# Stick-breaking attention inside a decoder block: the mask moves into the scan, and eight residual passes move behind the attention stage

## The chip, the cores and the metric

The kernel runs on one core of a Trainium2 chip. The metric is the device time of one execution in microseconds (us). The engines named below are TensorE (PE, matmuls; its weight loads are listed as PEld), VectorE (DVE), ScalarE (ACT), GpSimd (POOL) and SyncE (SP, which here only issues DMAs). Each engine works through its own queue of instructions in order; an instruction that waits holds up everything behind it on that engine, and nothing on the others unless they need its result.

## The reference

One decoder layer on 512 tokens of width 1024, in float32: a half-step SwiGLU feed-forward (width 2816), a token-mixing sublayer, and a second half-step feed-forward. Each is modulated by shift, scale and gate vectors from a conditioning vector, and followed by a LayerNorm over `alpha * x + gate * sublayer`. The token-mixing sublayer runs two branches from one input projection: stick-breaking attention (16 heads of 64) and a causal depthwise convolution of 31 taps. The two are projected, merged with sigmoid gates and projected again.

The change lies in the attention. Its core is

```
z = (q @ k.T) * scale
mask = s_idx < t_idx                      # strictly earlier tokens only
log_keep = where(mask, log_sigmoid(-z), 0)
between = reversed_cumsum(log_keep) - log_keep
w = where(mask, exp(log_sigmoid(z) + between), 0)
out = w @ v
```

So the weight of key `s` for query `t` is `sigmoid(z[t,s])` times the product of `sigmoid(-z[t,j])` over all `j` with `s < j < t`, and zero for `s >= t`.

## The kernel before

Tokens lie in four tiles of 128, the width in eight chunks of 128. Nearly all products are made in three matmuls: each float32 operand is split into a rounded high part and the remainder (`whi`/`wlo`, `uh`/`ul`, ...), and high*high, high*low and low*high are summed in PSUM.

The work runs in stages. The first feed-forward (with the modulation vectors beside it) ends at about 390 us. Then q, k, v and the convolution's inputs for the first heads are projected. From 423 to about 722 us the **attention stage** runs 64 units (8 pairs of heads x 2 heads x 4 query tiles `tb`) in a software pipeline. Step `i` of its loop (line 725) emits

- `att_scores(i)`: three matmuls into `z`; ACT writes `nb = sigmoid(-z)` (L629) and `be = sigmoid(z)` (L630); DVE runs a reversed multiplicative scan over `nb` (L631) that uses a constant tile `future`; POOL zeroes the masked part of `be` in its diagonal block with an affine select (L634) and multiplies `be` by the shifted `nb` (L636);
- some tasks of the input projection for later heads and for the convolution (`advance`), each a half of one weight tile;
- `att_values(i - 3)`: the products with v into `po` (L669 to L671);
- `att_transpose(i - 2)`: PE transposes of `be` into `pw` (L646), then ACT and DVE split them into `wTh` and `wTl` (L649, L650);
- two or three convolution taps on DVE (`bg`, L525), and on every fourth step one of the eight **slow** passes.

The slow passes come from `finish_x(1)` (line 302): over each of the four token tiles of the normalised residual `x`, POOL multiplies by a row `ln1_g * alpha` (four passes), and then adds a row `ln1_b * alpha` (four passes); L313 in the profile. The first pass of each four also fetches its row: a DMA on SP's queue (L100) that broadcasts 4 KB to 128 partitions of one of the three `raw` buffers, and an ACT multiplication by alpha (L307). The result is needed only when the sublayer's residual is added, near 930 us.

Weights of this sublayer come through `load_added` (line 125): SP loads a `raw` tile (3 buffers, shared with the two rows above), ACT rounds it into `whi` (L129) and writes `-whi` into `wlo` (L130), and a DMA on POOL's queue adds the source to `wlo` in flight (L131). `whi` and `wlo` have five buffers each, so a new weight is rounded when PE has finished with the one five before it.

After the attention, `parts_t(ysb)` splits the attention output (ACT L750, DVE L751), and the **first projection part** (loop at line 843, 40 tasks: gate `ga`, output projection `ysb`, half of gate `gb`, to 831 us) uses PE while DVE finishes the remaining taps. Then come the convolution's LayerNorm (`conv_normalize`, whose transposes L771 need every channel's last tap), its swish, its projection `ycv`, the merge and the output projection. The second feed-forward fills the rest.

The order of the instructions on each engine is not the program order as such. The kernel library's planner takes the trace of the program, and at each point gives an engine the earliest-traced instruction that it holds to be ready by its own cost estimates; buffers are handed out in that order too. `keep_in_program_order` ties one instruction behind the instruction traced just before it on the same engine, and nothing more: what follows in the program may still be put ahead of it, and it may be put ahead of everything else. It is used on the taps and on the slow passes' POOL instructions, not on the DMA and the ACT instruction that fetch a row.

Of the kernel before, what the change touches and what calls it, by code (L numbers as in the profile page):

```python
# [7 lines left out]
F32 = mybir.dt.float32  # L8
F32R = mybir.dt.float32r
BF16 = mybir.dt.bfloat16  # L10
AF = mybir.ActivationFunctionType
ALU = mybir.AluOpType
PSUM = bass.MemoryType.PSUM

P = 128
S = 512
D = 1024
KC = D // P
NT = S // P
# [11 lines left out]
LAG = 2  # L31
# [7 lines left out]
QSCALE = 0.125  # L39
# [3 lines left out]
def decoder_block(ctx: ExitStack, tc: tile.TileContext, a: dict, out: bass.AP):  # L43
    nc = tc.nc

    core = ctx.enter_context(tc.tile_pool(name="core", bufs=1))
# [3 lines left out]
    def open_pool(name, side="left", space=None):  # L50
        kw = {"space": space} if space is not None else {"side": side}
        cm = tc.tile_pool(name=name, bufs=1, reuse_waits="tile", **kw)
        return cm, cm.__enter__()

    def close_pool(cm):
        cm.__exit__(None, None, None)
# [7 lines left out]
    def bank(name, tag="ps"):  # L64
        return banks["pool"].tile([P, 512], F32, tag=tag, name=name, bufs=banks["bufs"][tag])
# [7 lines left out]
    ones = core.tile([P, P], F32, tag="uf", name="ones", bufs=2)  # L73
# [3 lines left out]
    ones_r = core.tile([P, P], F32R, name="ones_r")  # L77
    nc.vector.tensor_copy(ones_r, ones)

    future = core.tile([P, S], BF16, name="future")  # L80
    nc.gpsimd.memset(future[:, 0 : S - P], 0.0)
    nc.gpsimd.affine_select(future[:, S - P : S], ones, [[1, P]], ALU.is_ge, 0.0, base=0, channel_multiplier=-1)
    mhalf = core.tile([P, 1], F32, name="mhalf")
    nc.gpsimd.memset(mhalf, -0.5)

# [73 lines left out]
    def bg(n):  # L159
        for _ in range(min(n, len(background))):  # L160
            background.pop(0)()
# [140 lines left out]
    def finish_x(which):  # L302
        row = {}

        def fetch(v):
            row[v] = raw_tile(a[f"ln{which}_{v}"].broadcast_to([P, D]))
            nc.scalar.mul(row[v], row[v], ALPHA)  # L307

        def apply(t, v):
            if t == 0:  # L310
                fetch(v)
            op = nc.gpsimd.tensor_mul if v == "g" else nc.gpsimd.tensor_add
            tc.keep_in_program_order(op(x_t[t], x_t[t], row[v]))  # L313

        return [lambda t=t, v=v: apply(t, v) for v in "gb" for t in range(NT)]
# [184 lines left out]
    slow = finish_x(1)  # L500
# [6 lines left out]
    at_cm, ap_ = open_pool("mixa", "left")  # L507
# [104 lines left out]
        return [(fetch if t == 0 else None, lambda t=t: block(t)) for t in range(NT)]  # L612


    unit = {}

    def att_scores(i):
        j, hh, tb = i // 8, (i // 4) % 2, i % 4
        (qh, ql), (kh, kl) = qk[j, "q"], qk[j, "k"]
        rs = slice(hh * DH, (hh + 1) * DH)  # L620
        n = (tb + 1) * P
        tsl = slice(tb * P, (tb + 1) * P)
        z = bank("z", "z")
        nc.tensor.matmul(z[:, :n], qh[rs, tsl], kh[rs, :n], start=True, stop=False)  # L624
        nc.tensor.matmul(z[:, :n], qh[rs, tsl], kl[rs, :n], start=False, stop=False)
        nc.tensor.matmul(z[:, :n], ql[rs, tsl], kh[rs, :n], start=False, stop=True)
        nb = ap_.tile([P, S], F32, tag="nb", name="nb", bufs=2)
        be = ap_.tile([P, S], F32, tag="be", name="be", bufs=LAG + 1)
        nc.scalar.activation(nb[:, :n], z[:, :n], AF.Sigmoid, scale=-QSCALE)  # L629
        nc.scalar.activation(be[:, :n], z[:, :n], AF.Sigmoid, scale=QSCALE)  # L630
        nc.vector.tensor_tensor_scan(  # L631
            nb[:, 1:n][:, ::-1], nb[:, 1:n][:, ::-1],
            future[:, S - n + 1 : S][:, ::-1], 1.0, ALU.mult, ALU.max)
        nc.gpsimd.affine_select(be[:, n - P : n], be[:, n - P : n], [[-1, P]], ALU.is_gt, 0.0, base=0,  # L634
                                channel_multiplier=1)
        nc.gpsimd.tensor_mul(be[:, 0 : n - 1], be[:, 0 : n - 1], nb[:, 1:n])  # L636
        unit[i] = be

    def att_transpose(i):
        tb = i % 4  # L640
        n = (tb + 1) * P
        be = unit[i]
        pw = bank("pw", "pw")
        for sb in range(tb + 1):
            ss = slice(sb * P, (sb + 1) * P)
            nc.tensor.transpose(pw[:, ss], be[:, ss], ident)  # L646
        wh = ap_.tile([P, S], F32R, tag="wTh", name="wTh", bufs=2)
        wl = ap_.tile([P, S], F32R, tag="wTl", name="wTl", bufs=2)
        nc.scalar.copy(wh[:, :n], pw[:, :n])  # L649
        nc.vector.tensor_sub(wl[:, :n], pw[:, :n], wh[:, :n].bitcast(F32))  # L650
        unit[i] = (wh, wl)
# [3 lines left out]
    def att_values(i):  # L655
        j, hh, tb = i // 8, (i // 4) % 2, i % 4
        vh, vl = vq[j // 2]
        wh, wl = unit.pop(i)
        rs = slice(hh * DH, (hh + 1) * DH)
        vs = slice((j % 2) * P + hh * DH, (j % 2) * P + (hh + 1) * DH)  # L660
        tsl = slice(tb * P, (tb + 1) * P)
        if tb == 0:
            heads["po"] = bank("po", "po")
            if hh == 0:
                ysb.append(yp.tile([P, S], F32, tag="yF", name=f"yF{j}", bufs=KC))
        po = heads["po"]
        for sb in range(tb + 1):
            ss = slice(sb * P, (sb + 1) * P)
            nc.tensor.matmul(po[0:DH, tsl], vh[:, sb, vs], wh[:, ss], start=(sb == 0), stop=False)  # L669
            nc.tensor.matmul(po[0:DH, tsl], vh[:, sb, vs], wl[:, ss], start=False, stop=False)  # L670
            nc.tensor.matmul(po[0:DH, tsl], vl[:, sb, vs], wh[:, ss], start=False, stop=(sb == tb))  # L671
        if tb == NT - 1:
            nc.scalar.copy(ysb[j][rs, :], po[0:DH, :])
# [41 lines left out]
    def advance(to):  # L715
        nonlocal done, fetched
        while done < to:
            while fetched < min(done + AHEAD, len(tasks)):
                if tasks[fetched][0]:
                    tasks[fetched][0]()  # L720
                fetched += 1
            tasks[done][1]()
            done += 1

    for i in range(units + LAG + 1):
        if i < units:
            advance(max([done] + [x + 1 for x in range(done, len(tasks)) if need[x] <= i // 8]))
            att_scores(i)
        advance((i + 1) * len(tasks) // (units + LAG + 1))
        if i > LAG:  # L730
            att_values(i - LAG - 1)
        if LAG <= i < units + LAG:
            att_transpose(i - LAG)
        bg(int((i + 1) * CONV_PACE) - int(i * CONV_PACE))
        if i % 4 == 3 and slow:
            slow.pop(0)()
    close_pool(at_cm)

    t_cm, mp = open_pool("mixt", "left")
# [23 lines left out]
    def conv_normalize(t):  # L763
        tsl = slice(t * P, (t + 1) * P)
        st = bp.tile([P, 2, 6], F32, tag="cst", name="cst", bufs=2)
        n = [gp.tile([P, S], F32, tag="g", name="cn", bufs=NH_BUF) for _ in range(2)]
        pts = []
        for h in range(2):
            pt = bank("pt")
            for c in range(4):  # L770
                nc.tensor.transpose(pt[:, c * P : (c + 1) * P], cacc[4 * h + c][:, tsl], ident)  # L771
            nc.vector.bn_stats(st[:, h, :], pt)
            pts.append(pt)
        mv = bp.tile([P, 2], F32, tag="cmv", name="cmv", bufs=2)
        nc.vector.bn_aggr(mv, st)
        ve = bp.tile([P, 1], F32, tag="cve", name="cve", bufs=2)
        nc.vector.tensor_scalar_add(ve, mv[:, 1:2], EPS)
        rstd = bp.tile([P, 1], F32, tag="crs", name="crs", bufs=2)
        nc.gpsimd.tensor_tensor(rstd, ve, mhalf, ALU.pow)
        for h in range(2):  # L780
            nc.vector.tensor_scalar(n[h], pts[h], mv[:, 0:1], rstd, ALU.subtract, ALU.mult)
        normed[t] = n
# [47 lines left out]
    def advance_b(n):  # L830
        nonlocal done, fetched
        for _ in range(n):
            while fetched < min(done + AHEAD, len(queue)):
                if queue[fetched][0]:
                    queue[fetched][0]()
                fetched += 1
            queue[done][1]()
            done += 1
# [4 lines left out]
    for i in range(len(first_part)):  # L843
        advance_b(1)
        bg(min(n1, i + 1) * taps // n1 - min(n1, i) * taps // n1)
    assert not background
    conv_normalize(0)
    advance_b(1)
# [130 lines left out]
```

## Time and profile before

| | us |
|---|---|
| three runs | 1327.76, 1330.25, 1333.49 (median 1330.25) |
| the profiled execution, its own time | 1328.88 |
| its span in the trace | 1327.2 |
| PE busy in the span | 1292.2 |
| DVE, ACT, POOL busy in the span | 750.8, 524.6, 559.7 |

The profile lists instructions with their start and duration in us from the span's start. "Idle before" and a name behind `<-` give the time for which an engine did nothing ahead of an instruction, and the instruction or DMA that ended it. The granted clock (PEclk) is the share of full speed at which TensorE was allowed to run; a stretch at 0.50 takes twice as long for the same matmuls. The ends of matmuls are modelled, so neighbouring matmuls overlap in the list.

### The profile page before, as it was taken

Reading aid. Unit: us, or ns where it says so; the run is one execution under the profiler, and the core shown is the slowest. Engines: PE = TensorE matmul, PEld = TensorE weight load, DVE = VectorE, ACT = ScalarE, POOL = GpSimd, SP = SyncE. Lnnn points to the kernel's source line nnn. Section 1 sums busy time; section 2 is a strip of 40 time slices with the busy share of each in tenths; the row PEclk is TensorE's granted clock in tenths of the full one; section 3 lists DMA queues with packets and bytes.
Section 4 is the critical chain, followed back from the end, with each engine's and each line's share of the span. In section 5 each row is a group of like instructions: output and inputs, shape, how many; then the busy total and the mean of one; then the engine's idle time right before and its main releaser. Section 6 shows DMA issues by size and latency. Waiting matters only on the chain.

```text
span 1327.2 us, 16780 instructions
## 1 busy us (share of the span) xinstructions
PE 1292.2 (97%) x6444; PEld 1071.2 (81%) x6444; DVE 750.8 (57%) x1017; ACT 524.6 (40%) x794; POOL 559.7 (42%) x392
## 2 busy tenths in 40 slices
PE   6899999999999999999999999999999999999997
PEld 4688888888889878788778888878898888888885
DVE  7886885255462858766676876545672000025545
ACT  2233312222256555556556444852542222222220
POOL 2464535644222554534442111133264566564434
PEclk9999999999999989999999999999999999999999
DMA  9668886333327564655566989293273333323311
GB/s 356 217 211 314 293 293 215 103 96 96 95 81 171 123 150 96 159 112 118 121 135 135 191 193 200 51 225 109 77 272 100 101 106 101 117 96 96 96 64 63
DMA packets 57713, 197.36 MB, mean 149 GB/s; under 512 B 6673, under 2 KB 6817, under 8 KB 57633
## 3 DMA queue, kind: packets, MB, share of 16 engines
q1 hardware_dynamic: 47808, 160.63, 36.6%
q0 software_dynamic: 9824, 35.66, 16.4%
q8 instruction: 50, 0.82, 0.2%
q14 instruction: 31, 0.25, 0.1%
HBM read 194.17 MB, written 2.10 MB: 148 GB/s over the span
## 4 chain that ended last, share of the span: by engine, by line
PE 84%; DVE 8%; DMA 3%; issue 2%; ACT 1%; POOL 1%; SPq 0%; DVEq 0%; POOLq 0%; ACTq 0%
PE y L354 19%; DVE ada L188 3%; PE z L624 1%; DVE cacc L525 1%; PE pw L646 1%; PE glub L143 1%; PE ga L143 1%; PE ga L145 1%; PE ysb L145 1%; PE ga L144 1%; PE ysb L144 1%; PE ysb L143 1%; PE q L143 1%; PE glub L144 1%; PE glub L145 1%
## 5 line engine op out<-in xcount | busy, mean ns | idle before, releaser
L113 POOL TENSOR_TENSOR wlo<-raw,whi 128x1024 fp32r<-128x1024 f32 x88 | 224.8, 2561 | 239.0 <-ACT whi L112 233.5
L112 ACT CAST whi<-raw 128x1024 fp32r<-128x1024 f32 x144 | 149.6, 1046 | 265.3 <-DMA raw<-in_gu 45.2
L136 POOL TENSOR_TENSOR raw<-raw,mod_g 128x1024 f32<-128x1024 f32 x52 | 130.0, 2502 | 146.9 <-DMA raw<-in_dn 83.7
L525 DVE SCALAR_TENSOR_TENSOR cacc<-h,cv_w,cacc 128x512 f32<-128x512 f32 x232 | 179.7, 833 | 0.0
L129 ACT CAST whi<-raw 128x1024 fp32r<-128x1024 f32 x68 | 71.1, 1048 | 129.1 <-PE ysb L144 23.4
L113 DVE TENSOR_TENSOR wlo<-raw,whi 128x1024 fp32r<-128x1024 f32 x56 | 106.2, 1896 | 24.2 <-ACT whi L112 24.2
L354 PE MATMUL y<-whi,sh 128*128 128x512 f32 x352 | 113.8, 390 | 0.0
L354 PE MATMUL y<-wlo,sh 128*128 128x512 f32 x352 | 113.7, 389 | 0.0
L354 PE MATMUL y<-whi,sl 128*128 128x512 f32 x352 | 113.6, 389 | 0.0
L188 DVE SCALAR_TENSOR_TENSOR ada<-ada,crow 128x512 f32<-128x512 f32 x96 | 97.9, 1067 | 20.9 <-DMA ada<-in_ada_t 15.4
L418 DVE TENSOR_TENSOR sl<-sF,sh 128x512 fp32r<-128x512 f32 x44 | 45.3, 1031 | 85.3 <-ACT sh L417 85.3
L417 ACT CAST sh<-sF 128x512 fp32r<-128x512 f32 x44 | 27.1, 623 | 144.9 <-PE y L354 132.1
L131 POOL DMA_DIRECT2D wlo<-in_w_in x44 | 38.4, 872 | 98.9 <-ACT wlo L130 92.9
L636 POOL TENSOR_TENSOR be<-be,nb 128x127 f32<-128x127 f32 (+1 forms) x64 | 50.1, 783 | 68.7 <-DVE nb L631 55.1
L354 PEld LDWEIGHTS y<-whi,sl 128*128 128x128 f32 x352 | 66.1, 188 | 13.7
L354 PEld LDWEIGHTS y<-wlo,sh 128*128 128x128 f32 x352 | 66.1, 188 | 13.7
L354 PEld LDWEIGHTS y<-whi,sh 128*128 128x128 f32 x352 | 66.1, 188 | 13.5
L130 ACT ACTIVATE wlo<-whi 128x1024 fp32r<-128x1024 f32 x68 | 71.9, 1061 | 0.7
L650 DVE TENSOR_TENSOR wTl<-pw,wTh 128x128 fp32r<-128x128 f32 (+1 forms) x64 | 31.1, 485 | 52.8 <-ACT wTh L649 52.7
L634 POOL TENSOR_SCALAR_AFFINE_SELECT be<-be 128x128 f32<-128x128 f32 x64 | 40.9, 639 | 41.0 <-ACT be L630 40.6
L631 DVE TENSOR_TENSOR_SCAN nb<-nb,future 128x127 f32<-128x127 f32 (+1 forms) x64 | 53.4, 835 | 3.4 <-ACT nb L629 3.4
L221 DVE SCALAR_TENSOR_TENSOR acc<-ada,silu_c,acc 128x1024 f32<-128x1024 f32 x21 | 41.6, 1981 | 15.8 <-DMA ada<-in_ada_w 15.6
(494 smaller groups left out, 3376.4 us busy)
## 6 DMA issues: line engine op xcount, KB each, us to landing
raw<-in_gu SPq DMA_DIRECT2D x80, 512.0 KB, 3.6
raw<-in_w_in SPq DMA_DIRECT2D x48, 512.0 KB, 3.6
raw<-in_dn SPq DMA_DIRECT2D x44, 512.0 KB, 3.5
wlo<-in_w_in POOLq DMA_DIRECT2D x44, 512.0 KB, 6.0
ada<-in_ada_t SPq DMA_DIRECT2D x32, 512.0 KB, 5.3
ada<-in_ada_w SPq DMA_DIRECT2D x24, 512.0 KB, 5.0
ada<-in_ada SPq DMA_DIRECT2D x32, 256.0 KB, 6.0
raw<-in_gu_first SPq DMA_DIRECT2D x8, 512.0 KB, 6.6
```

What stands on the lines that cost most here:

```text
L112: nc.scalar.copy(hi, raw)
L113: lo_eng.tensor_sub(lo, raw, hi.bitcast(F32))
L129: nc.scalar.copy(hi, raw)
L130: nc.scalar.mul(lo, hi.bitcast(F32), -1.0)
L136: nc.gpsimd.tensor_mul(raw, raw, G)
L143: nc.tensor.matmul(ps[:, c0:c1], wh[:, ks], mov(uh, k)[:, c0:c1], start=(k == 0), stop=False)
L188: nc.vector.scalar_tensor_tensor(raw[:, qs], raw[:, qs], 1.0, crow[:, qs], ALU.mult, ALU.mult, accum_out=parts[:, q : q + 1])
L354: nc.tensor.matmul(acc[t][h][:, c0 - h * 512 : c1 - h * 512], st[:, tsl], wt[:, c0:c1], start=(k == 0 and i == 0 and c0 % 512 == 0), stop= ...
L418: nc.vector.tensor_sub(sl, sF[f], sh.bitcast(F32))
L525: ins = nc.vector.scalar_tensor_tensor(o, hv, cv_w[:, j, i : i + 1], o, ALU.mult, ALU.add)
L631: nc.vector.tensor_tensor_scan(nb[:, 1:n][:, ::-1], nb[:, 1:n][:, ::-1], future[:, S - n + 1 : S][:, ::-1], 1.0, ALU.mult, ALU.max)
L636: nc.gpsimd.tensor_mul(be[:, 0 : n - 1], be[:, 0 : n - 1], nb[:, 1:n])
```

## The change

Four edits.

1. The constant tile of the scan holds a one at the query's own token and zeros elsewhere (`own_token`, built with `is_equal`), where `future` held ones at the own token and everything behind it. The scan starts from 0 instead of 1. Running from the last key towards the first, its state is `max(state * nb, own_token)`: it stays 0 over the keys behind the query, becomes 1 at the query's own token and is multiplied by `nb` from there on. The product `be * nb` so is zero wherever the mask is, and the affine select (L634) is dropped.
2. `nb` and `be` are no longer taken from rings of 2 and 3 buffers of 512 columns. There is one `nb` and one `be` for each query tile, 128, 256, 384 and 512 columns wide, kept over the whole stage, so each is used every fourth unit. The total size is the same.
3. The last column of each `be` is set to zero once, before the stage, by four small memsets on POOL; ACT writes `be` without that column.
4. The slow passes are no longer emitted in the attention loop but in the first projection part, one after every second task (the first 16 of its 40).

The number of matmuls for a score is three before and after.

```diff
-    future = core.tile([P, S], BF16, name="future")
-    nc.gpsimd.memset(future[:, 0 : S - P], 0.0)
-    nc.gpsimd.affine_select(future[:, S - P : S], ones, [[1, P]], ALU.is_ge, 0.0, base=0, channel_multiplier=-1)
+    own_token = core.tile([P, S], BF16, name="own_token")
+    nc.gpsimd.memset(own_token[:, 0 : S - P], 0.0)
+    nc.gpsimd.affine_select(own_token[:, S - P : S], ones, [[1, P]], ALU.is_equal, 0.0, base=0, channel_multiplier=-1)
...
+    past = [ap_.tile([P, (tb + 1) * P], F32, name=f"nb{tb}") for tb in range(NT)]
+
+    weights = [ap_.tile([P, (tb + 1) * P], F32, name=f"be{tb}") for tb in range(NT)]
+    for tb in range(NT):
+        nc.gpsimd.memset(weights[tb][:, (tb + 1) * P - 1 :], 0.0)
     unit = {}
...
-        nb = ap_.tile([P, S], F32, tag="nb", name="nb", bufs=2)
-        be = ap_.tile([P, S], F32, tag="be", name="be", bufs=LAG + 1)
+        nb = past[tb]
+        be = weights[tb]
         nc.scalar.activation(nb[:, :n], z[:, :n], AF.Sigmoid, scale=-QSCALE)
-        nc.scalar.activation(be[:, :n], z[:, :n], AF.Sigmoid, scale=QSCALE)
+        nc.scalar.activation(be[:, : n - 1], z[:, : n - 1], AF.Sigmoid, scale=QSCALE)
         nc.vector.tensor_tensor_scan(
             nb[:, 1:n][:, ::-1], nb[:, 1:n][:, ::-1],
-            future[:, S - n + 1 : S][:, ::-1], 1.0, ALU.mult, ALU.max)
-        nc.gpsimd.affine_select(be[:, n - P : n], be[:, n - P : n], [[-1, P]], ALU.is_gt, 0.0, base=0,
-                                channel_multiplier=1)
+            own_token[:, S - n + 1 : S][:, ::-1], 0.0, ALU.mult, ALU.max)
         nc.gpsimd.tensor_mul(be[:, 0 : n - 1], be[:, 0 : n - 1], nb[:, 1:n])
         unit[i] = be
...
         bg(int((i + 1) * CONV_PACE) - int(i * CONV_PACE))
-        if i % 4 == 3 and slow:
-            slow.pop(0)()
     close_pool(at_cm)
...
     for i in range(len(first_part)):
         advance_b(1)
         bg(min(n1, i + 1) * taps // n1 - min(n1, i) * taps // n1)
+        if i % 2 and slow:
+            slow.pop(0)()
```

## The prediction

> **What bounds the kernel now.** I read the engines' totals first, then stretches around the stages that the change touches, then what PE waited for between 400 and 1000 us.
>
> ```profile
> PE 1292.2 (97%) x6444; PEld 1071.2 (81%) x6444; DVE 750.8 (57%) x1017; ACT 524.6 (40%) x794; POOL 559.7 (42%) x392
> ...
> 425.00:485.00 60.00, 59.71 (x369) 1.00 0.65 145
> 485.00:490.00 5.00, 2.49 (x16) 0.85 0.62 166
> 490.00:495.00 5.00, 5.00 (x16) 0.50 0.68 105
> 495.00:500.00 5.00, 5.00 (x26) 0.97 0.28 70
> 500.00:723.00 223.00, 221.76 (x1369) 1.00 0.58 124
> 723.00:831.00 108.00, 108.00 (x478) 1.00 0.88 190
> ...
> PE po L669 <- ACT wTh L649: 2.1, 1, 2.1
> PE po L670 <- DVE wTl L650: 1.3, 3, 0.5
> PE ga L143 <- ACT h L564: 0.7, 1, 0.7
> ```
>
> The first row is busy time by engine; the next six are stretch, length, PE busy (instructions), granted clock, DMA share and GB/s; the last three are who waited for whom: us in all, times, longest. PE is the bound: in the whole attention stage it is idle for 0.29 + 2.51 + 1.24 us, and POOL is nowhere named as the one that PE waits for. So this change, which takes nothing off PE, can win at most those gaps and the clock that one of them costs. Most of it is one place, so I followed that place across the queues:
>
> ```profile
> 479.37 5.28 DMA raw<-in_ln_b
> ...
> 484.67 1.06 ACT L307 ACTIVATE raw<-raw 128x1024 f32<-128x1024 f32 x1 [4.05 <-DMA raw<-in_ln_b]
> ...
> 487.66 0.57 ACT L649 CAST wTh<-pw 128x512 fp32r<-128x512 f32 x1
> ...
> 488.28 0.27 PE L669 MATMUL po<-wTh,vh 128*64 128x128 f32 x1 [2.06 <-ACT wTh L649]
> ```
>
> The second row of the residual passes is fetched in mid-attention. ACT stands 4.05 us in front of L307 until the row has landed; a weight's two conversions and the `wTh` cast (487.66) are queued behind it, and PE runs dry for 2.06 us, and right behind that comes its longest wait for `wTl` (the 0.5 above, 0.45 unrounded): the 2.51 of the stretch. Then the granted clock is down: (0.15 + 0.50 + 0.03) x 5 = **3.4 us** of work lost. A slow-pass row load, not the affine select, is what this stage pays for.
>
> [...]
>
> **The change part by part.**
>
> ```profile
> L634 POOL TENSOR_SCALAR_AFFINE_SELECT be<-be 128x128 f32<-128x128 f32 x64 | 40.9, 639 | 41.0 <-ACT be L630 40.6
> L636 POOL TENSOR_TENSOR be<-be,nb 128x127 f32<-128x127 f32 (+1 forms) x64 | 50.1, 783 | 68.7 <-DVE nb L631 55.1
> ...
> L313 POOL TENSOR_TENSOR n<-n,raw x8: 2360/2682/2850, 424.2 to 552.2; 128x1024 f32<-128x1024 f32 x8
> ...
> 472.25 1.41 DVE L525 SCALAR_TENSOR_TENSOR cacc<-h,cv_w,cacc 128x512 f32<-128x512 f32 x2
> 475.12 4.35 DVE L525 SCALAR_TENSOR_TENSOR cacc<-h,cv_w,cacc 128x512 f32<-128x512 f32 x2
> 476.08 2.84 POOL L313 TENSOR_TENSOR n<-n,raw 128x1024 f32<-128x1024 f32 x1
> ```
>
> *The affine select* (L634): 64 x 639 ns = 40.9 us leave POOL. The multiplication behind it waits 55.1 us for DVE's scan anyway, and PE waits for neither: 0 on the path. If that cover were gone, it would be 0.64 us of a unit's latency, not of throughput.
>
> *Scan, mask constant, one column less, buffers*: the scan is the same instruction on the same sizes with another start value; one column of 128 to 512 on ACT is nothing beside the 438 ns of L630; `nb` and `be` come back every fourth unit in place of every second and third, which can only take waits away, and no wait for them shows. 0.
>
> *The four memsets* stand once on POOL, where their tiles' memory was the first stage's:
>
> ```profile
> 389.23 0.23 POOL L563 MEMSET h<- 128x30 f32 x3
> 392.14 0.83 DVE n L273
> 396.39 0.91 POOL L131 DMA_DIRECT2D wlo<-in_w_v  x1 [4.29 <-ACT wlo L130]
> ```
>
> Four at 0.08 us each; the last reader of that memory (DVE's normalisation) is done at 392.97, and POOL idles for 4.29 us until 396.39. 0. Without that idle time the weight DMA behind them would be 0.3 us late, for products that start at 411 us.
>
> *The passes leave the attention.* DVE's taps stand still while POOL runs a pass: two taps took 4.35 us around the pass at 476 us, against 1.41 us just before, so 2.94 us. That delays the scan and `wTl`, and it explains the two other short waits for `wTl` (0.29 at 446 us, the idle time of 425 to 485; 0.55 at 558 us, which with the 0.7 of `ga` is the 1.24 of 500 to 723; each right behind a pass): -0.84 us. With the `ln_b` row the stall goes: -2.51 us and -3.4 us. The first row (`ln_g`, below) held ACT for 7.64 us, but at 415 to 423 us, before any unit, and PE had v products to do: 0.
>
> *Where they go.* A pass is tied only behind the POOL instruction traced before it. In the new place that is the weight DMA fetched one weight ahead, so pass 1 may follow the second weight's DMA, pass 8 the ninth's:
>
> ```profile
> 700.72 0.88 POOL L131 DMA_DIRECT2D wlo<-in_w_sb  x1 [2.36 <-ACT wlo L130]
> 723.51 0.86 POOL L131 DMA_DIRECT2D wlo<-in_w_in  x1 [5.94 <-ACT wlo L130]
> 746.62 0.87 POOL L131 DMA_DIRECT2D wlo<-in_w_in  x1 [4.23 <-ACT wlo L130]
> ```
>
> Counting the weights, three passes still fall into the attention's tail (behind 700.7, 710.7, 716.7 us) and five between 724 and 750 us. Three of eight passes cost 3/8 x 0.84 = +0.3 us. POOL itself idles 4 to 6 us ahead of each of these DMAs, more than a pass takes: 0. On DVE the five cost 5 x 2.94 = 14.7 us, and this is the cover:
>
> ```profile
> DVE ga L799 <- PE ysb L145: 16.6, 6, 5.0
> ...
> 823.73 0.69 DVE L530 TENSOR_TENSOR cacc<-cacc,cacc 128x512 f32<-128x512 f32 x1
> ...
> L771 PEld LDWEIGHTS pt<-ident,cacc x32: 138/141/143, 831.0 to 844.5; 128*128 128x128 f32 x32
> ```
>
> DVE waits 16.6 us in all for PE's `ysb` in this part, and has its last tap 6.6 us (831.0 - 824.4) before PE's transposes ask for it: 23.2 us of slack against 14.7. 0.
>
> *The two row loads move too*, through SP's queue and the three `raw` buffers. In order of tracing, `ln_g` comes between the second and third weight of the new part and takes the buffer free at 681.9 us; `ln_b` comes between the sixth and seventh and takes the one at 721.8.
>
> ```profile
> 681.91 0.33 SPq L100 DMA_DIRECT2D raw<-in_w_in  x1
> 721.79 0.33 SPq L100 DMA_DIRECT2D raw<-in_w_sb  x1
> DMA to landing us min/median/max: 3.7/6.0/10.4
> DMA to landing us min/median/max: 3.6/5.3/6.5
> ...
> 412.55 10.45 DMA raw<-in_ln_g
> 686.44 0.58 ACT L673 COPY yF<-po 64x512 f32<-64x512 f32 x1 [2.23 <-PE po L671]
> 687.04 0.27 ACT L649 CAST wTh<-pw 128x128 fp32r<-128x128 f32 x1
> 690.23 0.22 PE L669 MATMUL po<-wTh,vh 128*64 128x128 f32 x1
> 723.84 4.27 ACT L750 CAST ph<-yF 128x512 fp32r<-128x512 f32 x8
> L143 PE MATMUL ysb<-ph,whi x64: 388/389/390, 727.9 to 808.8; 128*128 128x512 f32 x64
> ```
>
> The two "to landing" rows are the three `ln_g` and the three `ln_b` loads of the kernel. Say L307 goes into ACT's 2.23 us gap, which begins at 684.2 us. With a landing of 5.3 us ACT is free at 681.9 + 5.3 + 1.06 = 688.3, casts the output copy (0.58) and `wTh` (0.27), done by 689.1; PE asks at 690.23: 0. Break-even is a landing of 6.4 us; at 10.45 it is 4.0 us of idling and, as at 488, 3.4 us of clock: +7.4. So 0 to 7.4; I take 0, since four of the six landings are under 6.4. `ln_b` lands about 727.1, while ACT does the eight casts of L750 (traced earlier, so preferred when ready) until 728.1: 0. If L307 stands ahead of them, the first cast (4.27 / 8) and its remainder (0.69, as DVE's operation of that size at 823.73) come 1.06 + 0.53 + 0.69 us behind the landing against 727.9: +1.5 us at 5.3, and +6.6 + 3.4 = +10.0 at 10.45. I take 0. Weights lose nothing: with one or, briefly, two of three raw buffers held, a weight's load mostly goes out two weights ahead, 11 us (four weights lie 23.1 us apart between 723.5 and 746.6), and the slowest of these six loads of the same 512 KB took 10.4.
>
> **Sum**: -2.51 - 3.4 - 0.84 + 0.3 = -6.4 us on the profiled execution of 1328.88, that is 1322.4. The median of the three runs is 1.4 us above that execution, so I state **1324**.
>
> **The rivals.**
>
> *A. The stall only moves to the attention's tail.* `ln_g` lands late at 682 us, with ACT in front of it. For: two of six landings exceed 6.4 us, and both early loads met ACT waiting. Against: 681.9 is in a stretch of moderate DMA load (0.58 share from 500 to 723). -6.4 + 7.4 = +1.0: **1331**.
>
> *B. Slower: ACT stands at the handoff.* At 722 to 734 us ACT must cast the attention output before any `ysb` product. If `ln_b`'s L307 is put ahead of L750, PE idles from a landing of 3.8 us on, and the whole is slower than before if that load takes over about 7 us. At 10.45: -6.4 + 10.0 = +3.6, **1334**. For: the planner put L307 at most 1.2 us behind the issue at 479. Against: earlier-traced work goes first.
>
> *C. DVE becomes the bound in the first projection part.* If the planner keeps all eight passes behind 722 us, DVE loses 8 x 2.94 = 23.5 us against 23.2 of slack. At the slowest tap seen (4094 ns, against 746 as the median, so 3.35 us a pass) it is 26.8: 3.6 us late and 3.4 of clock, +0.6 in all: **1331**.
>
> ```profile
> L525 DVE SCALAR_TENSOR_TENSOR cacc<-h,cv_w,cacc x232: 734/746/4094, 430.3 to 823.0; 128x512 f32<-128x512 f32 x116
> ```
>
> [...]
>
> *D. The change doesn't do what it says*: the planner may pull passes forward. It can't go far, since no row has landed before 686; the three passes above are that case.
>
> *E. More than the forecast*: the tail's three passes cost nothing and the 0.7 us wait at 722 us goes too: -7.4, **1322**; a reordered plan may shift gaps elsewhere too.
>
> **How the numbers follow.** Forecast 0.57, A 0.17, B 0.09, C 0.07, E 0.10 (D lies in the forecast). A measurement of this kernel can tell about 0.5% from no change (the three runs lie 0.43% apart), that is 6.7 us, so the bounds are 1323.6 and 1336.9. The forecast sits at the lower one: of its 0.57 I give 0.23 to faster and 0.34 to the same. E is 0.08 faster; A and C 0.22 the same, 0.02 slower; B 0.05 the same, 0.04 slower; 0.02 of E the same. Faster 0.31, the same 0.63, slower 0.06; as costs that I put at 0 may add up, I move 0.03 from the same to slower. The range reaches from 4 us below the forecast to B: 1320 to 1334; the forecast's own range is 1320 to 1328.
>
> **What would show it.** PE busy in 425 to 500 at 75 of 75 with a clock of 1.00, and no L307 between the units before 680. L313 at 700 to 750, with taps beside it of 3 to 4 us. `DVE ga <- PE ysb` down from 16.6 by some 10 us, and the last tap still ahead of L771. A PE gap of over 1 us near 685 to 690 is A, at 728 to 734 B, at 831 C. The forecast is wrong if the stretch 425 to 500 still has its gap, or if the whole gains over 8 us, which no gap of this stage could pay.

## The result, and the profile after

The changed kernel was timed twice against the kernel before. The six runs of the kernel before in the first row include the three of the table above; in the second row both kernels ran on one chip.

| | before, us | after, us | ratio, 95% interval |
|---|---|---|---|
| first | 1327.53 (6 runs) | 1321.42 (6 runs, 1320.62 to 1322.90) | 0.9947 (0.9927 to 0.9967) |
| again | 1327.62 (12 runs) | 1322.63 (7 runs, 1320.20 to 1326.07) | 0.9967 (0.9954 to 0.9979) |

So it is faster by 5 to 6 us, about 0.4%: a real gain, and about as large as what a measurement of this kernel can tell. 1324 was forecast.

The engines' totals and the same stretches of PE as in the prediction (stretch, length, PE busy, granted clock, DMA share, GB/s), then what PE waited for between 400 and 1000 us, all of the changed kernel:

```profile
PE 1286.9 (98%) x6444; PEld 1067.1 (81%) x6444; DVE 757.2 (57%) x1017; ACT 525.1 (40%) x794; POOL 524.9 (40%) x332
...
425.00:500.00 75.00, 75.00 (x461) 1.00 0.63 135
680.00:723.00 43.00, 41.37 (x230) 1.00 0.60 132
723.00:831.00 108.00, 108.00 (x491) 1.00 0.90 199
860.00:880.00 20.00, 16.95 (x73) 1.00 1.03 259
...
PE ycv L145 <- DMA wlo<-in_w_cv: 3.0, 2, 2.3
PE po L673 <- DVE wTl L653: 0.9, 1, 0.9
PE ga L143 <- ACT h L564: 0.7, 1, 0.7
```

The gap at 485 us is gone, with the half clock behind it: 75 of 75 us busy at 1.00. The wait for `wTh` has left the list, and of the three waits for `wTl` one is left. The gate's wait of 0.7 us and the 3 us for the weights of the convolution's projection (`w_cv`, 860 us) are as before, the latter now as two waits of 2.3 and 0.7 us.

The moved work in its new place (passes on POOL, row loads on SP with the time to landing of the three `ln_g` and the three `ln_b` loads, the two multiplications by alpha on ACT, and DVE's wait for `ysb`, its last tap and PE's transposes behind it):

```profile
L313 POOL TENSOR_TENSOR n<-n,raw x8: 2692/2716/2732, 693.9 to 741.1; 128x1024 f32<-128x1024 f32 x8
...
L100 SPq DMA_DIRECT2D raw<-in_ln_g x2: 328/328/328, 674.5 to 1035.3; - x2
DMA to landing us min/median/max: 3.3/3.4/6.4
L100 SPq DMA_DIRECT2D raw<-in_ln_b x2: 327/328/328, 715.7 to 1082.2; - x2
DMA to landing us min/median/max: 3.3/3.7/6.4
...
677.85 1.06 ACT L307 ACTIVATE raw<-raw 128x1024 f32<-128x1024 f32 x1 [1.03 <-DMA raw<-in_ln_g]
721.90 1.05 ACT L307 ACTIVATE raw<-raw 128x1024 f32<-128x1024 f32 x1
...
DVE ga L800 <- PE ysb L145: 5.0, 1, 5.0
817.62 0.69 DVE L530 TENSOR_TENSOR cacc<-cacc,cacc 128x512 f32<-128x512 f32 x1
L772 PEld LDWEIGHTS pt<-ident,cacc x32: 138/140/142, 824.9 to 838.4; 128*128 128x128 f32 x32
```

The attention now ends some 6 us earlier (first `ga` product at 716.2 us against 722.3), so the places correspond to those of the prediction less 6. Three passes run before 716 us and five behind. `ln_g` landed in 3.3 us: ACT waited 1.03 us in its gap, and PE not at all. `ln_b`'s multiplication (721.90) stands behind the eight casts of the handoff, which end at 722.0, and waits for nothing. DVE waits for `ysb` 5.0 us in place of 16.6 and still has its last tap 6.6 us early.

### The profile page after: what moved, and what is told of

It reads as the page before. It is cut to its first block, busy times and chain, and to the rows that moved or that the text cites. A ratio compares the mean times of both kernels' runs of the same rounds, so it can differ in the third digit from the quotient of the medians.

```text
span 1319.0 us, 16657 instructions
## 1 busy us (share of the span) xinstructions
PE 1286.9 (98%) x6444; PEld 1067.1 (81%) x6444; DVE 757.2 (57%) x1017; ACT 525.1 (40%) x794; POOL 524.9 (40%) x332
## 4 chain that ended last, share of the span: by engine, by line
PE 89%; DVE 7%; DMA 1%; POOL 1%; ACT 1%; issue 1%; SPq 0%; DVEq 0%; POOLq 0%; ACTq 0%
PE y L354 19%; DVE ada L188 3%; PE z L629 2%; PE pw L649 1%; PE psv L600 1%; PE k L143 1%; PE q L143 1%; PE glua L143 1%; PE psv L601 1%; PE psv L602 1%; PE glub L143 1%; PE ga L143 1%; PE gb L145 1%; PE gb L143 1%; PE ysb L143 1%; PE gb L144 1%
## 5 line engine op out<-in xcount | busy, mean ns | idle before, releaser
L113 POOL TENSOR_TENSOR wlo<-raw,whi 128x1024 fp32r<-128x1024 f32 x88 | 222.1, 2531 | 241.8 <-ACT whi L112 228.4
L525 DVE SCALAR_TENSOR_TENSOR cacc<-h,cv_w,cacc 128x512 f32<-128x512 f32 x232 | 182.9, 847 | 0.0
L636 DVE TENSOR_TENSOR_SCAN nb<-nb,own_token 128x127 f32<-128x127 f32 (+1 forms) x64 | 52.1, 815 | 4.5 <-ACT nb L634 4.5
L460 PE MATMUL first<-uh,whi 128*128 128x512 f32 x64 | 27.2, 425 | 18.5 <-ACT whi L112 18.5
```

Of the source, the lines that this page charges most:

```text
L113: lo_eng.tensor_sub(lo, raw, hi.bitcast(F32))
L525: ins = nc.vector.scalar_tensor_tensor(o, hv, cv_w[:, j, i : i + 1], o, ALU.mult, ALU.add)
L636: nc.vector.tensor_tensor_scan(nb[:, 1:n][:, ::-1], nb[:, 1:n][:, ::-1], own_token[:, S - n + 1 : S][:, ::-1], 0.0, ALU.mult, ALU.max)
```

## The experiments

The theory: the whole gain is the `ln_b` row load, which ACT waited for in mid-attention, together with the clock that PE lost behind it, and the mask edit is worth nothing. First rival: dropping the affine select shortens the chain and gives a part. Second rival: not the row load but POOL's passes, which hold up DVE, made the gap. A further question is whether the cover in the new place was luck: how many more passes would it bear?

### The mask edit alone

```diff
     # the changed kernel, but:
+        if i % 4 == 3 and slow:      # in the attention loop, as before
+            slow.pop(0)()
...
-        if i % 2 and slow:           # in the first projection part
-            slow.pop(0)()
```

> The mask edit alone: scan with own_token, no affine select, kept nb and be tiles, memsets; the slow passes stay in the attention loop. Theory (the gain is the ln_b row load that left the attention): no gain, ratio 0.999 to 1.001 to the kernel before, the PE gap near 485 us and the half clock behind it still there (PE busy about 72 of 75 us from 425 to 500). Rival (the shorter chain without the affine select gives part of it): at least 2 us faster, ratio 0.9985 or less, with no change at the gap.

Measured: 1327.26 against 1327.68 us, ratio 0.9998 (0.9987 to 1.0009). The stretch of the attention and the waits of PE:

```profile
425.00:500.00 75.00, 72.91 (x435) 0.98 0.66 143
485.00:490.00 5.00, 2.91 (x19) 0.90 0.63 144
490.00:495.00 5.00, 5.00 (x21) 0.76 0.48 85
...
PE po L672 <- ACT wTh L652: 1.6, 1, 1.6
PE po L673 <- DVE wTl L653: 0.9, 2, 0.5
```

The gap is still there (POOL's passes wait 11.5 us in all for L307 in this trace, against 7.64 + 4.06 = 11.7 in the one before), and the mask edit without the move is worth nothing. The first rival falls.

In this execution the same gap cost less than in the one of the prediction: 2.09 us of idle PE and (0.10 + 0.24) x 5 = 1.7 us of clock, 3.8 us in all against 5.9. The price of the gap is not one number; the last section comes back to it.

### The passes alone

```diff
     # the kernel before, but:
-        if i % 4 == 3 and slow:      # in the attention loop
-            slow.pop(0)()
...
+        if i % 2 and slow:           # in the first projection part
+            slow.pop(0)()
```

> The passes alone: mask, affine select and rings of buffers as before; the slow passes in the first projection part as after the change. Theory: the whole gain, ratio about 0.995 (-6 us), PE busy 75 of 75 us from 425 to 500. Rival (the affine select gives part): at most half of it, ratio 0.9975 or more.

Measured: 1323.04 us, ratio 0.9971 (0.9961 to 0.9981), -4.6 us. That is between the two expectations, and less than the change had given in its first timing. The trace places the difference. Up to the convolution's projection the two are the same: the first `ga` product starts at 716.3 (after the change: 716.2), the first `ycv` product at 854.1 (854.0), and the attention's stretch is at 75 of 75. Then the same gap for the `w_cv` weight follows in both, and behind it the clock differs. Of the passes alone, and then of the changed kernel run once more:

```profile
860.00:870.00 10.00, 7.36 (x20) 0.69 1.05 244
870.00:880.00 10.00, 10.00 (x44) 0.97 1.02 259
```

```profile
860.00:870.00 10.00, 7.37 (x31) 1.00 1.03 237
870.00:880.00 10.00, 10.00 (x46) 1.00 1.05 287
```

2.6 us of idle PE each, yet one execution loses (0.31 + 0.03) x 10 = 3.4 us of clock (what of it fell in PE's idle time is counted twice) and the other none.

### The changed kernel again, and with the select put back

```diff
     # the changed kernel, and with it (the second of the two kernels):
+        nc.gpsimd.affine_select(be[:, n - P : n], be[:, n - P : n], [[-1, P]], ALU.is_gt, 0.0, base=0,
+                                channel_multiplier=1)
         nc.gpsimd.tensor_mul(be[:, 0 : n - 1], be[:, 0 : n - 1], nb[:, 1:n])
```

> The changed kernel itself once more, as the measure for the three others on the same chip and to see whether the passes alone really fell short of it. Theory (the mask edit is worth nothing, and the difference between the passes alone, 0.9971, and the change, 0.9947, is the clock behind a gap in the convolution's projection): ratio 0.994 to 0.998 to the kernel before, not clearly apart from the passes alone. Rival (mask edit and passes help each other): 0.9947 or less again.

> The changed kernel with the affine select put back ahead of each multiplication, where it zeroes what the scan zeroes already; tiles, scan and passes as after the change. Theory: the select's 0.64 us a unit is hidden behind the scan, so within 1 us of the changed kernel. Rival (the select costs what the passes alone lacked): 1.5 us or more slower than the changed kernel.

Measured: 0.9967 (0.9954 to 0.9979) for the changed kernel and 0.9964 (0.9952 to 0.9977) with the select put back. The passes alone had 0.9971. The three can't be told apart: 64 affine selects on POOL cost nothing here, and the lower 0.9947 of the first timing was not a joint effect of the two parts.

### The passes kept in the attention, without their row loads

```diff
     # the kernel before, but:
         def apply(t, v):
-            if t == 0:
+            if which == 1:
+                row[v] = mods["g2"]          # resident since the first stage
+            elif t == 0:
                 fetch(v)
...
             att_scores(i)
+            if i % 4 == 3 and slow:          # tied behind this unit's multiplication
+                slow.pop(0)()
...
-        if i % 4 == 3 and slow:              # at the end of the step, as before
-            slow.pop(0)()
```

> The kernel before, with its eight passes still in the attention (one tied behind every fourth unit's multiplication) but multiplying and adding a resident row (the second gate) in place of the two loaded rows, so that the two row loads and their ACT multiplications are left out; the residual is therefore another one. Theory (the row load that ACT waits for costs 2.5 us of idle PE and 3.4 us of clock): -5.5 to -6 us, ratio about 0.9955, granted clock 1.00 from 425 to 500; what the passes' hold on DVE costs (0.8 us) stays. Rival (the gap comes from POOL's passes holding up DVE): no gain, ratio 0.999 or more, gaps of PE behind the passes.

Measured: 1321.20 us, ratio 0.9956 (0.9941 to 0.9971), -5.8 us by the ratio. Its passes and the attention's stretches:

```profile
L315 POOL TENSOR_TENSOR n<-n,mod_g x8: 2396/2828/2867, 440.2 to 561.6; 128x1024 f32<-128x1024 f32 x8
...
425.00:500.00 75.00, 75.00 (x460) 1.00 0.65 137
500.00:680.00 180.00, 179.44 (x1123) 1.00 0.56 121
```

All eight passes still run between 440 and 562 us, as long as before; without the loads the gap and the lost clock are gone, and the kernel is as fast as after the change. The one wait left there, 0.6 us (180.00 - 179.44), is what the passes' hold on DVE costs. So the row load is the cause, and the second rival falls. Two things go with the load in this kernel and were not tried apart from it: ACT's multiplication of the row (1.06 us) is left out too, and each pass is emitted earlier in its step. The queue of ACT in the trace before (4.05 us of waiting for the row, then 1.06 us of work) says that most of it is the wait.

### Sixteen passes in the new place

```diff
     # the changed kernel, but:
     slow = finish_x(1)
+    slow += [lambda t=t: tc.keep_in_program_order(nc.gpsimd.tensor_mul(x_t[t], x_t[t], mods["g2"]))
+             for _ in range(2) for t in range(NT)]
```

> The changed kernel with eight more passes of the same size behind the eight, one after every second task, multiplying x by a resident row (the residual is therefore another one). Theory (POOL's pass holds DVE up for 2.9 us each, and the first projection part has cover for the eight only): 8 x 2.94 = 23.5 us more of DVE against about 12 us of cover left, so the last tap comes some 11 us too late for the transposes; with the clock behind such a gap +11 to +15 us over the changed kernel, about 1333 to 1336. Rival (the hold is hidden anyway): within 1 us of the changed kernel, about 1321.

Measured: 1332.34 us, ratio 1.0038 (1.0025 to 1.0052): slower than the kernel before, and 10 to 11 us slower than the changed kernel. PE's wait for the tap's sum, DVE's last tap, and the stretches of PE behind it:

```profile
PE pt L774 <- DVE cacc L532: 7.3, 1, 7.3
...
832.63 0.69 DVE L532 TENSOR_TENSOR cacc<-cacc,cacc 128x512 f32<-128x512 f32 x1
...
831.00:860.00 29.00, 26.63 (x141) 0.91 0.12 19
860.00:870.00 10.00, 9.91 (x44) 1.00 0.35 109
870.00:880.00 10.00, 5.60 (x14) 0.70 1.04 239
```

The cover is real and has an end. Eight more passes moved the last tap from 818.3 to 833.3 us and used up the 5.0 us wait for `ysb` on the way: 20.0 us, or 2.5 us a pass. PE waited 7.3 us for it (some 11 by the expectation, which had 2.94 us a pass), and lost clock at 831 to 860 ((1 - 0.91) x 29 = 2.6 us) and again behind the `w_cv` weight.

### A step further: the weights behind the convolution

The one large wait left, 3 us at 860 us, is of the same kind: something that PE needs stands late in ACT's queue. In the changed kernel ACT rounds the second `w_cv` weight at 855 us, behind the whole swish and its casts. Two kernels try it.

```diff
     # first kernel: the changed one, but:
     assert not background
+    while fetched < len(queue):              # the gates' weights stay ahead
+        if queue[fetched][0]:
+            queue[fetched][0]()
+        fetched += 1
+    for j in range(2):
+        early[j] = load_added(a["w_cv"][j])  # proj_tasks uses early[j] where there is one
     conv_normalize(0)
...
     # second kernel: also
     def gate_done(name, j, ps):
+        # for gb, j >= 4: append the sigmoid to `held` and do nothing else
...
     cp2 = parts_t(cacc)
+    for finish in held:
+        finish()
```

> A further step from the changed kernel: the first two weights of the convolution's projection are traced ahead of the convolution's normalisation, so that ACT rounds the second one before the swish and not behind it. PE there waits 3 us for that weight's DMA, and the clock falls behind that wait in most runs (0.83 to 0.91 of 20 us). Theory (a weight that comes late behind ACT's work): the wait goes, 3 to 5 us faster than the changed kernel, about 1317. Rival (ACT is full there, and what it does earlier makes the swish and the casts behind it late): the wait only changes its name, within 1 us of the changed kernel.

> As the kernel with the two early weights, and the last four gates' sigmoids are emitted behind the swish, which saves ACT most of its changes between the swish's and the sigmoid's tables (1.28 us each). Theory (ACT is the late one there): faster than with the early weights alone by 1 to 3 us, and 4 to 6 us faster than the changed kernel, about 1316. Rival: no faster than the early weights alone, since PE waits for the weights and not for ACT.

Measured: 1319.43 us (0.9946, 0.9934 to 0.9958) with the early weights, 3.2 us less than the changed kernel on the same chip, though the two intervals touch; and 1316.81 us (0.9924, 0.9911 to 0.9937; 1316.56 to 1316.99) with the held sigmoids as well, 5.8 us less than the changed kernel and 10.8 less than the kernel before. PE at 860 us, first with the early weights, then with both:

```profile
860.00:880.00 20.00, 19.07 (x84) 1.00 0.97 248
```

```profile
860.00:880.00 20.00, 20.00 (x90) 1.00 0.98 252
```

The wait shrinks to 0.9 us and then goes, and no clock is lost behind it. The rival of the early weights has a part in it: ACT's last cast of the swish now ends at 859.3 us in place of 855.3, and the first `ycv` product starts at 855.4 in place of 854.0. The second kernel beats both: its four runs lie 0.4 us apart and all below those of the others. Its ACT changes tables four times between 825 and 880 us in place of six (1.28 us each), so fewer changes were saved than expected, and its last cast ends at 851.9 us. Whether the saved changes or the new order of ACT's work gave the 2.6 us was not tried apart.

## Why the prediction was right

**What bounds it.** As it was put: PE, with one gap in the attention that this change can pay. The kernel without row loads shows the gap's cause, with the two reservations above, and the two kernels on the select show that none of POOL's 40.9 us was on the path.

**The sum.** The prediction had -6.4 us for the profiled execution, 1322.4; the profiled execution after took 1321.83. By places, from the first score product to the first `ga` product: 423.0 to 722.3 us before and 422.7 to 716.2 after, so 5.8 us less. The terms -2.51, -3.4 and -0.84 came as put, within some 0.2 us (0.2 of the 3.4 counts idle time again: from 488.55 to 489.00 us PE stood idle at a clock of 0.50); the three passes left in the attention's tail cost 0.94 us (one wait for `wTl`) in place of 0.3. That makes -5.81. The whole span shrank by 8.2 us (1327.2 to 1319.0; the executions' own times differ by 7.05): 0.3 ahead of the first score product, 5.8, and 2.1 behind the first `ga` product. Most of the 2.1 is clock at 860 us, where the execution before lost 0.09 x 20 = 1.8 us and the one after none:

```profile
860.00:880.00 20.00, 17.00 (x68) 0.91 0.84 215
```

That is not the change's doing. So the mechanism was right, but how well the number fits is in part luck: the sum took the gap at the 5.9 us of one execution, and with the mask edit alone it was 3.8. The second timing, 5.0 us, lies between. The 1322 of the sum was better than the 1324 that was stated: the 1.4 us added for the median came from three runs, and with more runs the median before is 1327.5, under the profiled execution and not above it.

**Costs put at nothing.** The memsets ran at 391.9 us in POOL's idle time:

```profile
391.90 0.20 POOL L619 MEMSET be<- 128x1 f32 x4
```

Weights were in time: PE was busy 108 of 108 us from 723 to 831. DVE's cover held, and its size was about right: the wait for `ysb` fell by 11.6 us ("some 10 us" in the prediction), against 14.7 us charged for five passes. The charge of 2.94 us a pass was too high: the sixteen passes gave 2.5.

**The rivals.** A: the place was right (L307 did go into ACT's gap, at 677.85 us) but the load landed in 3.3 us, so the break-even of 6.4 us was not reached. B: the planner put `ln_b`'s multiplication behind the casts (L750 before, L751 after), as argued. C: three passes ran before 716 us, so the eight never met the cover together; with sixteen the mechanism came, and PE waited 7.3 us for the last tap. E: the wait of 0.7 us at 722 us stayed (on the base of the other rivals, 1330.25 - 7.4, its time would have been 1323).

**The clock behind the gap.** The half clock followed a gap of 2.51 us at 485 us in the kernel before, where it held for 6.83 us (488.48 to 495.31 us in windows of 0.1 us), and one of 2.09 us with the mask edit alone, where it held for 3.4 us ((0.10 + 0.24) x 5 us lost, at 0.50). So the prediction's 3.4 us is the loss of one execution, not of the gap. It is also a little high as a sum: in the kernel before, `glub` products of one shape start every 0.226 us ahead of the gap (484.70 to 485.83 us) and every 0.425 us at 0.50 (493.20 to 494.90 us), 1.9 times as far apart and not twice. By these two numbers the 6.83 us would have cost 3.2 (an estimate).

## What to carry to other kernels

An in-order engine that feeds the bound engine should not hold an instruction whose operand is still on its way: what the load cost here was not its bytes (the same 512 KB held PE up nowhere in the new place), but the 4.05 us for which ACT stood in front of work that was ready: 2.51 us of idle PE and 3.4 us of clock. The planner may put it there by itself: here ACT stood at L307 from 1.2 us behind the issue of a load that took 5.3 us. Why the planner did so (probably too early an estimate of the landing) stays open. When PE's busy share is 97%, look for the few places where it idles and read the granted clock just behind them, since the second number can be larger than the first (3.4 us against 2.51 here). Work moved off a critical stage needs a counted cover in its new place: here eight passes fit and sixteen made the kernel slower than before.

## What the runs showed of the hardware

The clock lost behind one and the same gap is not one number. The gap for the `w_cv` weights is there in eight of the ten traces (the changed kernel has two), with 2.6 to 3.4 us of idling (4.5 with sixteen passes). The granted clock, in windows of 0.1 us in the kernel before and of 10 us in the others, gives how long it stood at 0.50 behind that gap:

| half clock | traces |
|---|---|
| none | changed kernel, changed kernel again |
| 3.4 us (1.7 us of clock) | before, mask edit alone, passes kept without row loads |
| 6.8 us (3.4 us of clock) | passes alone, select put back, sixteen passes |

The same reading gives 6.8 us for the gap at 485 us in the kernel before and 3.4 us there with the mask edit alone (windows of 5 us). Behind the 7.3 us wait of the sixteen passes it gives 5.2 us from 831 us on (0.91 of 29 us); what lay ahead of 831 us is not told apart. In the other ten gaps it was 0, 3.4 or 6.8 us, each to about 0.2 us, and nothing between. In the kernel before, the half clock began 2.3 us after PE fell idle at 486.2 us, 0.2 us after PE had work again, and 2.9 us after PE fell idle at 867.9 us, just before it had work (870.78 against 870.80 us).

What decides whether a gap loses none, one or two times 3.4 us was not shown: 2.6 us of idling were followed by no half clock in the changed kernel again, and by 6.8 us of it with the passes alone.

The same gap in two executions of nearly the same kernel so differs by up to 3.4 us. The kernel before, with two gaps of that kind, scatters over 7 us (1323.71 to 1331.07 in 25 runs), while the last kernel, which has neither, scatters over 0.4 in its four runs. The kernels between them, with one gap, scatter over 1.5 us (6 runs, without row loads) to 5.9 us (7 runs, the changed kernel again); the numbers of runs differ too much to say more.

Nor is a row load one number: the same 512 KB broadcast took from 3.3 to 10.4 us to land in the traces before and after the change.
